# Gated delta rule in steps of 128 tokens instead of 64, in a hybrid mixer kernel

## The chip, the cores and the metric

The kernel runs on one core of one Trainium2 chip. The metric is the device time of one execution in microseconds (us); lower is better. The time before is 1988.86 us, the median of three runs (1986.17 to 1990.41).

## The reference

One layer of a decoder trunk works on 1024 tokens of width 1024. An input projection feeds five branches (gated DeltaNet, spatial gating, sparse attention, Mamba-2, cross-attention); their outputs are projected, gated and summed. The change lies in the first branch alone, in its gated delta rule, which has 4 heads of key and value width 128:

```
S_t = a_t S_{t-1} (I - b_t k_t k_t^T) + b_t v_t k_t^T,   o_t = S_t q_t
per chunk:  a_mat = I + tril(beta * (k k^T) * decay, -1)
            w_k, u0 = a_mat^-1 [beta * exp(gc) * k,  beta * v]
            u = u0 - w_k S;   o = (q * exp(gc)) S + (q k^T * decay) u
            S = exp(gc_last) S + (k * exp(gc_last - gc))^T u
```

Here gc is the running sum of the log decays within a chunk. The reference uses chunks of 64 tokens (16 of them); the recurrence itself does not depend on the size of the chunk.

## The kernel before, in words

Tokens lie in NT = 8 blocks of 128, and each block holds two chunks of 64, one in partitions 0 to 63 and one in 64 to 127 (E64). `branch_a` (L576) goes over the heads at L766. For each head there are these parts:

- `front(h)` (L614) makes the three projections q, k and v: each is 16 steps of three fp32r matmuls with 512 columns (`gin`), 48 steps in all, each projection followed by a convolution on ScalarE and VectorE. `proj_steps` is a generator, and `front(h+1)` is drawn on while head h is worked on: `feed(n)` (L623) issues n steps of three matmuls at that point of the program. For the last head the filling is `gate_steps(4)` (L567, tile `gate`), matmuls of the same form.
- `decays(h)` (L594) loads the rows of decays and betas by DMA on SyncE's queue (`dec`, `br`, `qd`, L598 to L601) and makes the factors of the chunk's matrix. `dec` has two buffers and `br` one of its own, so that the loads for the next head can come early.
- `mid(h)` (L623) first transposes and normalises q and k (L637 to L664), then makes the matrix U and its diagonal block inverse X with its transpose Y, and doubles the inverse four times (L687): each round is three groups of 16 matmuls of 64x64 (`prod`, L586; tiles `t`, `xt`, `t2y`), two at a time in opposite quarters of the array, with VectorE between them. L700 to L709 join the 32-token blocks into the transposed inverse `yb` of each 64-token chunk. L712 to L717 make `wk`.
- The scan (L722 to L741) takes 16 steps. Each step has five small products: `pu` from `yb` and `vb`, `pu` from `wk` and the state, `pst` from `kd` and `u`, `po` from `qd` and the state, `po` from `dec` and `u`; ScalarE copies `u` and `o`, and VectorE makes the next state `st` (L735). `feed(1)` stands behind the copy of `u`.
- `finish(h)` (L744) norms the output, makes one more projection (`a_gate`) and stores.

An fp32 product shows in the trace as two matmul instructions; an fp32r product is one.

The work is written as a dataflow; the framework that builds the program fixes the order of each engine's instructions beforehand, by their place in the program and by modelled times, and an instruction written later can be pulled forward into a place where its engine would stand idle. So `gate` matmuls that only head 3 draws stand in head 0 already. Within an engine's queue, and within SyncE's queue of DMA issues, the order is then fixed. The top-k rounds of the sparse attention (MAX8 and MATCH_REPLACE8 on VectorE) are spread over the VectorE instructions of branch a and of two later stages (`topk`, L474, with `share` at L1082), as work that fills gaps.

Of the kernel before, what the change touches and what calls it, by code (L numbers as in the profile page):

```python
# [15 lines left out]
P = 128  # L16
D = 1024
L = 1024
NT = L // P
# [36 lines left out]
def mixer_body(ctx, tc, a, out):  # L56
    nc = tc.nc
    S, G = nc.scalar, nc.gpsimd
    V, T = Traced(nc.vector), Traced(nc.tensor)
# [3 lines left out]
    px = ctx.enter_context(ExitStack())  # L63
# [10 lines left out]
    def gps(name, tag="g"):  # L74
        return pp.tile([P, 512], F32, name=name, tag=tag, bufs=banks[tag])

    def sps(name):
        return gps(name, "s")
# [91 lines left out]
    ekd = keep.tile([P, NT, 4], F32, name="ekd")  # L170
    cda = keep.tile([P, NT, 2, 4], F32, name="cda")
    btok = keep.tile([P, NT, 4], F32, name="btok")
    bte = keep.tile([P, NT, 4], F32, name="bte")
# [30 lines left out]
    HF = (slice(0, 4), slice(4, 8))  # L204

    def r3(t, c=P):
        return t.rearrange("p (n c) -> p n c", c=c)

    def flat(t):
        return t.rearrange("p n c -> p (n c)")  # L210

    def b3(ap, n, c=P):
        return ap[:, :, None].to_broadcast([P, n, c])
# [32 lines left out]
    with tc.tile_pool(name="xin", bufs=1, side="right") as xp:  # L246
# [6 lines left out]
        for b in range(8):  # L253
            ps = gps("gkvm", "f")
# [76 lines left out]
    def scores(name, q, j, kh, kl, c0, n):  # L331

        ps = sps(name)
        qj = q[:, j * P:(j + 1) * P]
        T.matmul(ps[:, :n], qj, kh[:, c0:c0 + n], start=True, stop=False)
        T.matmul(ps[:, :n], qj, kl[:, c0:c0 + n], start=False, stop=True)
        return ps
# [25 lines left out]
    with tc.tile_pool(name="idx", bufs=1, reuse_waits="tile") as ip:  # L363
        w = [split(*w_tiles("w"), raw[:, k:k + 4]) for k in (0, 4)]
        mraw = ip.tile([P, L], F32, name="mraw")
        for hv in HV:
            ps = gps("gmisc")
# [4 lines left out]
        z, sp, e, w, pl = r16("z"), r16("sp"), r16("e"), r16("w"), r16("pl")  # L372
# [24 lines left out]
        for hf in HF:  # L397
            ps = sps("ldT")
# [11 lines left out]
        ps = sps("csT")  # L410
# [6 lines left out]
        ps = sps("last")  # L417
# [17 lines left out]
        br = ip.tile([8, L], F32, name="br", tag="br")  # L435
# [12 lines left out]
        for c0 in range(0, L, 512):  # L448
            ps = sps("ikd")
# [4 lines left out]
        for b in range(4):  # L454
            th = stacks(ip, proj_in(OFF["c_iq"] + b * P), "iqs", 3)
            for j in range(NT):
                for hf in range(2):
                    h = 2 * b + hf
                    W = P * (j + 1)
                    for c0, n in cuts(W):  # L460
                        ps = scores("ix", th[hf], j, ikh, ikl, c0, n)
# [114 lines left out]
    def branch_a(gp):  # L576
        t3 = lambda nm, tg, b=1: gp.tile([P, NT, P], F32, name=nm, tag=tg, bufs=b)
        c3 = lambda nm, b=1: gp.tile([P, NT, 64], F32, name=nm, tag=nm, bufs=b)
        yb = t3("yb", "yb")
        G.memset(yb, 0.0)  # L580
        csv = csd.rearrange("r (j e c) -> r e j c", j=NT, e=2)
        btv = btd.rearrange("r (j e c) -> r e j c", j=NT, e=2)
        E64 = [slice(0, 64), slice(64, 128)]
# [8 lines left out]
        ready = []  # L592

        def decays(h):  # L594
            dec = c3("dec", 2)
            br = c3("br")
            for e in range(2):
                nc.sync.dma_start(dec[E64[e]], csv[h, e].partition_broadcast(64))  # L598
                nc.sync.dma_start(br[E64[e]], btv[h, e].partition_broadcast(64))
            qd = t3("qd", "qd")  # L600
            nc.sync.dma_start(flat(qd), egd[h].partition_broadcast(P))  # L601

            V.tensor_tensor(dec, dec, b3(cs[:, :, h], NT, 64), OP.subtract)
            nb = gp.tile([P, NT, 64], F32, name="nb", tag="T2c", bufs=1)
            V.tensor_scalar(nb, dec, 0.0, None, OP.max)
            V.tensor_scalar(dec, dec, 0.0, None, OP.min)
            S.activation(flat(nb), flat(nb), AF.Exp, scale=-1.0)
            S.activation(flat(dec), flat(dec), AF.Exp)
            G.tensor_tensor(br, br, dec, OP.mult)
            G.tensor_tensor(nb, nb, b3(btok[:, :, h], NT, 64), OP.mult)  # L610
            G.tensor_tensor(nb, nb, lv(0), OP.mult)
            return dec, br, nb, qd
# [10 lines left out]
        def mid(h, more, ch3, dec, br, nb, qd):  # L623
            def feed(n, after=False):
                with ExitStack() as x:
                    if after:
                        x.enter_context(tc.issue_after(T.log[-1]))
                    for _ in range(n):
                        next(more, None)
# [3 lines left out]
            rk = gp.tile([P, NT], F32, name="rk", tag="rk", bufs=2)  # L633
            kn = t3("kn", "T2")
            vb = t3("vb", "vb")
            kps = []
            for hf in HF:  # L637
                ps = tr4("kT", lambda i: ch3["k"][:, hf.start + i, :])
# [4 lines left out]
            for hf in HF:  # L643
                ps = tr4("vT", lambda i: ch3["v"][:, hf.start + i, :])
# [7 lines left out]
            knT = t3("knT", "knT")  # L652
            for hf in HF:
                ps = tr4("knTp", lambda i: kn[:, hf.start + i, :])
                S.activation(flat(knT[:, hf]), ps, AF.Copy)
            for hf in HF:
                ps = tr4("qT", lambda i: ch3["q"][:, hf.start + i, :])
# [5 lines left out]
            kd = t3("kd", "kd")  # L663
            G.tensor_tensor(kd, kn, b3(ekd[:, :, h], NT), OP.mult)  # L664

            U = c3("U")
            X, Y = c3("X"), c3("Y")
            idb = idl[:, None, :].to_broadcast([P, NT, 64])
            ps = sps("kk")
            prod(ps, lambda j, e: knT[:, j, e], lambda j, e: knT[:, j, e])  # L670
            V.tensor_tensor(flat(U), ps, flat(br), OP.mult)
            V.tensor_tensor(X, r3(ps, 64), nb, OP.mult)
            V.tensor_tensor(X, idb, X, OP.subtract)
            V.tensor_tensor(Y, U, lv(6), OP.mult)
            V.tensor_tensor(Y, idb, Y, OP.subtract)
            feed(1)
            ps = sps("kq")
            prod(ps, lambda j, e: knT[:, j, e], lambda j, e: ch3["q"][:, j, e])
            V.tensor_tensor(flat(dec), ps, flat(dec), OP.mult)
            for e in E64:  # L680
                G.affine_select(dec[e], dec[e], pattern=[[0, NT], [1, 64]], compare_op=OP.is_ge, fill=0.0, base=0, channel_multiplier=-1)
            for hf in HF:
                V.tensor_tensor(qd[:, hf], qd[:, hf], ch3["q"][:, hf], OP.mult)
            feed(1)

            T2 = c3("T2c")
            for k in range(1, 5):  # L687
                ps = sps("t2")
                prod(ps, lambda j, e: U[e, j, :], lambda j, e: X[e, j, :])
                V.tensor_tensor(T2, r3(ps, 64), lv(k), OP.mult)  # L690
                feed(2)
                px = sps("xt2")
                prod(px, lambda j, e: Y[e, j, :], lambda j, e: T2[e, j, :])
                py = sps("t2y")
                prod(py, lambda j, e: T2[e, j, :], lambda j, e: Y[e, j, :])
                V.tensor_tensor(flat(X), flat(X), px, OP.subtract)
                V.tensor_tensor(flat(Y), flat(Y), py, OP.subtract)
                feed(2, h < 2)

            Q = [(slice(0, 32), slice(32, 64)), (slice(64, 96), slice(96, 128))]  # L700
            ps, py = sps("t2"), sps("t2y")
            for i, (e, (r0, r1)) in enumerate(zip(E64, Q)):
                S.activation(yb[e, :, e], Y[e], AF.Copy)
                for j in range(NT):
                    T.matmul(ps[r1, j * 32:(j + 1) * 32], U[r0, j, 32:64], X[r0, j, 0:32], start=True, stop=True)
                S.activation(T2[r1, :, 0:32], r3(ps[r1, 0:256], 32), AF.Copy)
                for j in range(NT):
                    T.matmul(py[r0, j * 32:(j + 1) * 32], T2[r1, j, 0:32], Y[r1, j, 32:64], start=True, stop=True)
                V.tensor_tensor(yb[r0, :, r1], Y[r0, :, 32:64], r3(py[r0, 0:256], 32), OP.subtract)  # L709
            feed(2)  # L710

            wk = t3("wk", "knT")  # L712
            for hf in HF:
                ps = sps("wkp")
# [4 lines left out]
            st = gp.tile([P, P], F32, name="st", tag="st", bufs=2)  # L719
            G.memset(st, 0.0)  # L720
            o = t3("o", "T2")
            for n in range(16):  # L722
                j, ei = divmod(n, 2)
                e = E64[ei]
                pu = sps("pu")
                T.matmul(pu[e, 0:P], yb[e, j, e], vb[e, j, :], start=True, stop=False)
                T.matmul(pu[e, 0:P], wk[:, j, e], st, start=False, stop=True)
                u = gp.tile([P, P], F32, name="u", tag="u", bufs=2)
                S.activation(u[e], pu[e, 0:P], AF.Copy)
                feed(1)  # L730
                if n < 15:
                    pst = sps("pst")
                    T.matmul(pst[:, 0:P], kd[e, j, :], u[e], start=True, stop=True)
                    s2 = gp.tile([P, P], F32, name="st", tag="st", bufs=2)
                    V.scalar_tensor_tensor(s2, st, cda[:, j, ei, h:h + 1], pst[:, 0:P], OP.mult, OP.add)  # L735
                po = sps("po")
                T.matmul(po[e, 0:P], qd[:, j, e], st, start=True, stop=False)
                T.matmul(po[e, 0:P], dec[e, j, :], u[e], start=False, stop=True)
                S.activation(o[e, j, :], po[e, 0:P], AF.Copy)
                if n < 15:  # L740
                    st = s2  # L741
            return o, rq

# [360 lines left out]
    fill = []  # L1104
# [229 lines left out]
    with tc.tile_pool(name="fo", bufs=1, reuse_waits="tile") as fo:  # L1334
# [8 lines left out]
        for j in range(4):  # L1343
            tok = [slice((j + 4 * i) * P, (j + 4 * i + 1) * P) for i in range(2)]
            base = []
# [33 lines left out]
```

## Time and profile before

| | |
|---|---|
| median of 3 runs | 1988.86 us |
| the profiled execution's own time | 1991.76 us |
| its span, first to last instruction | 1989.8 us |
| TensorE busy / weight load busy | 95% / 75% |
| VectorE / ScalarE / GpSimd busy | 77% / 39% / 27% |
| mean granted TensorE clock | 0.986 |
| head 0 of branch a: preparing and inverse, scan, finish | 203.20 to 254.58, to 299.30, to 313.50 us |
| scans of heads 1, 2, 3 | 362.00 to 406.30, 462.30 to 508.30, 563.80 to 608.80 us |

How to read it: PE is TensorE's matmuls, PEld its weight loads (which overlap with matmuls), DVE is VectorE, ACT ScalarE, POOL GpSimd, SPq the DMA issues of SyncE. A matmul's shown duration is longer than what it occupies of the engine, since matmuls are pipelined; what a run of them occupies is read from the distance of their starts. Nearly all matmuls and VectorE instructions are recorded under L50, a line of the helper that logs them, so the tile names tell them apart.

### The profile page before, as it was taken

To read this page: it belongs to the slowest core of one execution; us is meant where nothing else is said; L and a number is where in the kernel's file an instruction comes from. 1 tells how busy PE (TensorE), PEld (TensorE's weight loads), DVE (VectorE), ACT (ScalarE), POOL (GpSimd) and SP (SyncE) were. 2 spreads that over 40 slices of the span, in tenths; PEclk is the share of its full clock that TensorE was granted. 3 is DMA by queue.
4 is the path that set the end of the run, shared out by engine and by line. 5 is a ranking of instruction groups with operands and counts; after the bars stand their busy time and mean duration, and the time that the engine had idled before them with its cause. 6 is when DMAs were issued, how large, how long until landed. Compare 5 with 4: busy or idle time off the path is not lost.

```text
span 1989.8 us, 30429 instructions
## 1 busy us (share of the span) xinstructions
PE 1885.3 (95%) x11116; PEld 1486.7 (75%) x11116; DVE 1533.0 (77%) x2699; ACT 780.9 (39%) x1511; POOL 545.6 (27%) x513
## 2 busy tenths in 40 slices
PE   6999999999999999969999999999989989999888
PEld 5777757676667787758888888888867667887767
DVE  7678958686846899798777787777787758897874
ACT  6465332323223341334222233343333737764231
POOL 5102202020200313443222222222115254444134
PEclk9999999999999999979999999999999999999999
DMA  6413102020202221233333333333368363324533
GB/s 191 116 48 70 44 17 59 17 60 17 61 31 69 53 55 48 85 100 117 106 106 117 111 111 108 109 113 112 108 219 288 126 188 104 97 86 139 170 110 132
DMA packets 187910, 199.89 MB, mean 100 GB/s; under 512 B 23641, under 2 KB 139214, under 8 KB 187762
## 3 DMA queue, kind: packets, MB, share of 16 engines
q1 hardware_dynamic: 187186, 196.91, 32.1%
q8 instruction: 88, 1.44, 0.3%
q10 hardware_dynamic: 576, 1.05, 0.1%
q14 instruction: 60, 0.49, 0.1%
HBM read 141.67 MB, written 52.05 MB: 97 GB/s over the span
## 4 chain that ended last, share of the span: by engine, by line
PE 68%; DVE 12%; issue 4%; DMA 3%; POOL 2%; ACT 2%; SPq 0%; POOLq 0%; DVEq 0%; ACTq 0%
PE pm L50 30%; PE gin L50 12%; PE proj L50 6%; PE po L50 4%; PE gate L50 2%; PE lg L50 2%; PE pT L50 2%; DVE cacc L50 1%; PE pu L50 1%; PE pst L50 1%; PE t L50 1%; DMA yr<-yd 1%; PE t2y L50 1%; DVE sc L50 1%; DVE m L50 1%
## 5 line engine op out<-in xcount | busy, mean ns | idle before, releaser
L50 PE MATMUL proj<-part,whi 128*128 128x512 f32 x640 | 210.6, 404 | 8.2 <-DVE tgl L50 3.1
L50 DVE MAX8 m<-sc 128x8 f32<-128x384 f32 (+5 forms) x192 | 170.4, 888 | 1.6
L50 DVE MATCH_REPLACE8 sc<-m,sc 128x384 f32<-128x384 f32 (+5 forms) x192 | 168.1, 876 | 0.0
L105 ACT ACTIVATE fh<-fs 128x512 fp32r<-128x512 f32 x132 | 83.1, 632 | 193.6 <-PE pm L50 187.8
L50 PEld LDWEIGHTS proj<-part,whi 128*128 128x128 f32 x640 | 121.1, 192 | 34.9 <-DVE tgl L50 4.6
L50 PE MATMUL proj<-part,wlo 128*128 128x512 f32 x320 | 128.8, 403 | 4.8 <-DVE wlo L50 4.8
L50 DVE SCALAR_TENSOR_TENSOR u<-pm,u 128x512 f32<-128x512 f32 x128 | 85.0, 684 | 47.5 <-PE pm L50 47.2
L105 ACT ACTIVATE whi<-wraw 128x512 fp32r<-128x512 f32 x106 | 66.4, 629 | 138.3 <-PE gin L50 88.9
L105 ACT ACTIVATE fh<-gr 128x512 fp32r<-128x512 f32 x90 | 56.8, 632 | 146.4 <-PE pm L50 115.3
L50 DVE TENSOR_TENSOR fl<-fs,fh 128x512 fp32r<-128x512 f32 x132 | 93.8, 713 | 3.5 <-ACT fh L105 3.5
L1154 POOL TENSOR_TENSOR fs<-gr 128x512 f32<-128x512 f32 x30 | 38.9, 1297 | 184.7 <-DVE fl L50 182.2
L1300 POOL TENSOR_TENSOR mg<-mg,tgl 128x512 f32<-128x512 f32 x48 | 67.9, 1417 | 57.4 <-DVE tgl L50 51.0
L50 DVE TENSOR_TENSOR fl<-gr,fh 128x512 fp32r<-128x512 f32 x90 | 64.1, 713 | 24.5 <-ACT fh L105 24.5
L50 DVE SCALAR_TENSOR_TENSOR cacc<-craw,pc,cacc 128x1023 f32<-128x1023 f32 (+2 forms) x60 | 77.6, 1294 | 6.3 <-ACT cacc L543 5.9
L50 DVE TENSOR_TENSOR wlo<-wraw,whi 128x512 fp32r<-128x512 f32 x82 | 59.6, 731 | 29.4 <-ACT whi L105 19.5
L50 DVE SCALAR_TENSOR_TENSOR st<-st,cda,pst 128x128 f32<-128x128 f32 x60 | 20.8, 347 | 74.4 <-PE pst L50 74.3
L50 PEld LDWEIGHTS proj<-part,wlo 128*128 128x128 f32 x320 | 61.2, 191 | 17.1 <-DVE wlo L50 5.2
L1153 POOL TENSOR_TENSOR fs<-gr 128x512 f32<-128x512 f32 x30 | 39.5, 1317 | 117.3 <-issue 117.3
L877 ACT ACTIVATE lg<-lg,mx,rq 128x128 f32<-128x128 f32 (+7 forms) x64 | 54.9, 861 | 18.5 <-DVE mx L50 16.3
L50 DVE SCALAR_TENSOR_TENSOR lg<-sc,cf,lg 128x384 f32<-128x384 f32 (+3 forms) x96 | 56.3, 605 | 6.9 <-POOL cf L856 3.8
L50 PE MATMUL pm<-h00h,fl 128*128 128x512 f32 x120 | 47.8, 398 | 12.4 <-DVE fl L50 12.4
L50 DVE SCALAR_TENSOR_TENSOR sc<-rl,iwt,sc 128x512 f32<-128x512 f32 (+3 forms) x84 | 47.1, 615 | 13.1 <-ACT rl L463 11.8
(579 smaller groups left out, 5714.1 us busy)
## 6 DMA issues: line engine op xcount, KB each, us to landing
tgl<-gd SPq DMA_DIRECT2D x80, 256.0 KB, 3.0
wraw<-in_w_in_dram SPq DMA_DIRECT2D x66, 256.0 KB, 2.9
gr<-in_w_gate_dram SPq DMA_DIRECT2D x32, 512.0 KB, 3.6
gr<-in_w_in_dram SPq DMA_DIRECT2D x28, 512.0 KB, 3.8
yr<-yd SPq DMA_DIRECT2D x40, 256.0 KB, 3.8
wraw<-in_w_branch_dram SPq DMA_DIRECT2D x40, 256.0 KB, 3.9
yd<-sg SPq DMA_DIRECT2D x16, 512.0 KB, 3.1
gd<-u SPq DMA_DIRECT2D x30, 256.0 KB, 3.8
```

Of the source, the lines that this page charges most:

```text
L50: r = f(*args, **kw)
L105: S.activation(hi, raw, AF.Copy)
L877: S.activation(lg[:, :W], lg[:, :W], AF.Exp, scale=rq[:, 2 * j + hf:2 * j + hf + 1], bias=mx[:, hf:hf + 1], accum_out=sm[:, hf:hf + 1])
L1153: eng.tensor_tensor(s3, a11, a21, OP.subtract)
L1154: eng.tensor_tensor(s1, a21, a22, OP.add)
L1300: (G if n < 4 else V).tensor_tensor(m, m, t, OP.add)
```

## The change

The scan goes over the 8 blocks of 128 tokens. The two 64-token chunks of a block become one chunk of 128, for which these things are needed:

- The factors `bte`, `ekd` and the block's decay `cdc` become products of the two chunks' decays (five small VectorE instructions, once).
- The lower left quarter of the inverse of the 128-token matrix (its transpose stands in the upper right quarter of `yb`): a further doubling, of two groups of 8 unpaired 64x64 products with VectorE's factor between them and a ScalarE copy behind, and 8 more 32x32 products that complete X.
- The products of the second chunk's queries and keys with the first chunk's keys (`px`, 16 products of 128x64, put into round 3 of the doubling), scaled on VectorE into `dq` (128x128 per block, takes the place of `dec` in the scan) and `UX`.
- `qd` of the second chunk is multiplied by the first chunk's decay, on GpSimd.
- `dec` keeps one buffer instead of two, and X shares the one buffer of `br` (tag `br`).
- `feed` is called with 2 in each of the 8 steps of the scan instead of with 1 in each of 16, and with 2 at two more places behind the joining.

```
     def branch_a(gp):
-        yb = t3("yb", "yb")
+        yb, dq = t3("yb", "yb"), t3("dq", "dq")
         G.memset(yb, 0.0)
+        G.memset(dq, 0.0)
+        hbt, hkd, cdc = [gp.tile([P, NT, 4], F32, name=nm) for nm in ("hbt", "hkd", "cdc")]
+        V.tensor_copy(hbt, bte)
+        V.tensor_copy(hkd, ekd)
+        V.tensor_tensor(bte[64:128], hbt[64:128], cda[64:128, :, 0, :], OP.mult)
+        V.tensor_tensor(ekd[0:64], hkd[0:64], cda[0:64, :, 1, :], OP.mult)
+        V.tensor_tensor(cdc, cda[:, :, 0, :], cda[:, :, 1, :], OP.mult)
...
-            dec = c3("dec", 2)
+            dec = c3("dec")
...
-            U = c3("U")
-            X, Y = c3("X"), c3("Y")
+            e0, e1 = E64
+            U, UX, Y = c3("U"), c3("UX"), c3("Y")
+            X = gp.tile([P, NT, 64], F32, name="X", tag="br", bufs=1)
...
-                G.affine_select(dec[e], dec[e], pattern=[[0, NT], [1, 64]], ...)
-            for hf in HF:
-                V.tensor_tensor(qd[:, hf], qd[:, hf], ch3["q"][:, hf], OP.mult)
+                G.affine_select(dq[e, :, e], dec[e], pattern=[[0, NT], [1, 64]], ...)
...
+            hk = hkd[e0, :, h:h + 1].to_broadcast([64, NT, 64])
             for k in range(1, 5):
+                if k == 2:
+                    for hf in HF:
+                        V.tensor_tensor(qd[:, hf], qd[:, hf], ch3["q"][:, hf], OP.mult)
+                if k == 3:
+                    px = sps("kqx")
+                    for j in range(NT):
+                        T.matmul(px[e0, j * 64:(j + 1) * 64], knT[:, j, e0], qd[:, j, e1], start=True, stop=True)
+                        T.matmul(px[e1, j * 64:(j + 1) * 64], knT[:, j, e0], knT[:, j, e1], start=True, stop=True)
+                    V.tensor_tensor(dq[e0, :, e1], r3(px, 64)[e0], hk, OP.mult)
+                    V.tensor_tensor(UX[e0], r3(px, 64)[e1], hk, OP.mult)
+                    G.tensor_tensor(qd[:, :, e1], qd[:, :, e1], b3(cda[:, :, 0, h], NT, 64), OP.mult)
...
+                if i == 0:
+                    for j in range(NT):
+                        T.matmul(py[r1, j * 32:(j + 1) * 32], Y[r1, j, 32:64], T2[r1, j, 0:32], start=True, stop=True)
+                    S.activation(X[r1, :, 0:32], r3(py[r1, 0:256], 32), AF.Copy, scale=-1.0)
...
+            feed(2)
+            ps = sps("t2")
+            for j in range(NT):
+                T.matmul(ps[e1, j * 64:(j + 1) * 64], UX[e0, j, :], X[e0, j, :], start=True, stop=True)
+            V.tensor_tensor(T2[e1], r3(ps, 64)[e1], hbt[e1, :, h:h + 1].to_broadcast([64, NT, 64]), OP.mult)
+            feed(2)
+            py = sps("t2y")
+            for j in range(NT):
+                T.matmul(py[e0, j * 64:(j + 1) * 64], T2[e1, j, :], yb[e1, j, e1], start=True, stop=True)
+            S.activation(yb[e0, :, e1], r3(py, 64)[e0], AF.Copy, scale=-1.0)
             feed(2)
...
-            for n in range(16):
-                j, ei = divmod(n, 2)
-                e = E64[ei]
+            for n in range(NT):
                 pu = sps("pu")
-                T.matmul(pu[e, 0:P], yb[e, j, e], vb[e, j, :], start=True, stop=False)
-                T.matmul(pu[e, 0:P], wk[:, j, e], st, start=False, stop=True)
+                T.matmul(pu[:, 0:P], yb[:, n, :], vb[:, n, :], start=True, stop=False)
+                T.matmul(pu[:, 0:P], wk[:, n, :], st, start=False, stop=True)
                 u = gp.tile([P, P], F32, name="u", tag="u", bufs=2)
-                S.activation(u[e], pu[e, 0:P], AF.Copy)
-                feed(1)
-                if n < 15:
+                S.activation(u, pu[:, 0:P], AF.Copy)
+                feed(2)
+                if n < NT - 1:
                     pst = sps("pst")
-                    T.matmul(pst[:, 0:P], kd[e, j, :], u[e], start=True, stop=True)
+                    T.matmul(pst[:, 0:P], kd[:, n, :], u, start=True, stop=True)
                     s2 = gp.tile([P, P], F32, name="st", tag="st", bufs=2)
-                    V.scalar_tensor_tensor(s2, st, cda[:, j, ei, h:h + 1], pst[:, 0:P], OP.mult, OP.add)
+                    V.scalar_tensor_tensor(s2, st, cdc[:, n, h:h + 1], pst[:, 0:P], OP.mult, OP.add)
                 po = sps("po")
-                T.matmul(po[e, 0:P], qd[:, j, e], st, start=True, stop=False)
-                T.matmul(po[e, 0:P], dec[e, j, :], u[e], start=False, stop=True)
-                S.activation(o[e, j, :], po[e, 0:P], AF.Copy)
+                T.matmul(po[:, 0:P], qd[:, n, :], st, start=True, stop=False)
+                T.matmul(po[:, 0:P], dq[:, n, :], u, start=False, stop=True)
+                S.activation(o[:, n, :], po[:, 0:P], AF.Copy)
```

## Rows read from the trace of the kernel before

**Rows 1.** The page's first part: busy us, share of the span, instructions.

```profile
PE 1885.3 (95%) x11116; PEld 1486.7 (75%) x11116; DVE 1533.0 (77%) x2699; ACT 780.9 (39%) x1511; POOL 545.6 (27%) x513
```

**Rows 2.** Busy time by stretch: head 0's inverse, then the four scans.

```profile
core 0: us, PE busy (x) PEld busy (x) DVE busy (x) ACT busy (x) POOL busy (x), PEclk, DMA share, GB/s
203.20:254.58 51.38, 49.83 (x667) 40.33 (x667) 45.55 (x88) 15.85 (x28) 11.03 (x7) 1.00 0.16 43
254.58:299.30 44.72, 44.72 (x222) 23.90 (x221) 21.75 (x48) 15.08 (x42) 3.01 (x4) 1.00 0.07 19
362.00:406.30 44.30, 44.30 (x221) 23.88 (x221) 22.51 (x45) 15.83 (x44) 2.97 (x4) 1.00 0.08 18
462.30:508.30 46.00, 45.98 (x228) 24.83 (x227) 28.99 (x60) 15.62 (x43) 3.77 (x4) 1.00 0.07 18
563.80:608.80 45.00, 45.00 (x223) 24.01 (x223) 14.29 (x31) 13.44 (x40) 0.00 (x0) 1.00 0.11 36
```

**Rows 3.** The scans, filling alone: four rows of tile gin, then one of gate.

```profile
254.58:299.30 44.72, 23.30 (x65) 10.24 (x65) 0.00 (x0) 2.44 (x4) 1.00 0.07 19
362.00:406.30 44.30, 22.91 (x64) 10.25 (x65) 0.00 (x0) 2.61 (x5) 1.00 0.08 18
462.30:508.30 46.00, 24.53 (x71) 11.21 (x71) 0.00 (x0) 2.33 (x4) 1.00 0.07 18
563.80:608.80 45.00, 4.70 (x13) 2.16 (x14) 0.00 (x0) 0.00 (x0) 1.00 0.11 36
...
563.80:608.80 45.00, 18.55 (x51) 8.01 (x51) 1.77 (x3) 1.00 0.11 36
```

**Rows 4.** Timeline of TensorE, one scan step of head 0: start, duration, what.

```profile
258.81 0.48 PE L50 MATMUL pst<-u,kd 64*128 64x128 f32 x2
259.23 0.43 PE L50 MATMUL po<-st,qd 128*64 128x128 f32 x2
259.59 0.32 PE L50 MATMUL po<-u,dec 64*64 64x128 f32 x1
259.60 0.32 PE L50 MATMUL pu<-vb,yb 64*64 64x128 f32 x1
...
259.96 0.50 PE L50 MATMUL gin<-h01h,wlo 128*128 128x512 f32 x1
...
260.62 0.43 PE L50 MATMUL pu<-st,wk 128*64 128x128 f32 x2
...
261.64 0.48 PE L50 MATMUL pst<-u,kd 64*128 64x128 f32 x2
```

**Rows 5.** Timeline of TensorE, head 0 ahead of the scan: five places.

```profile
193.34 0.39 PE L50 MATMUL gin<-h00l,whi 128*128 128x512 f32 x1
...
195.83 0.39 PE L50 MATMUL gin<-h10h,whi 128*128 128x512 f32 x1
...
216.64 1.15 PE L50 MATMUL kk<-knT 128*64 128x64 f32 x32
...
245.81 0.69 PE L50 MATMUL t<-X,U 32*32 32x32 f32 x16
...
252.69 1.96 PE L50 MATMUL wkp<-yb,kb 128*128 128x128 f32 x16
```

**Rows 6.** Weight loads by tile: duration in ns min/median/max, first and last start.

```profile
L50 PEld LDWEIGHTS pu<-st,wk x32: 132/134/136, 254.9 to 298.2; 128*64 128x64 f32 x32
...
L50 PEld LDWEIGHTS wkp<-yb,kb x16: 187/192/192, 252.6 to 254.3; 128*128 128x128 f32 x16
```

**Rows 7.** Timeline of VectorE: one product of the inverse, one state update.

```profile
223.18 0.68 DVE L50 TENSOR_TENSOR T2c<-t,lvl 128x512 f32<-128x512 f32 x1
...
259.34 0.35 DVE L50 SCALAR_TENSOR_TENSOR st<-st,cda,pst 128x128 f32<-128x128 f32 x1 [2.25 <-PE pst L50]
```

**Rows 8.** Timeline of SyncE's DMA issues in head 0.

```profile
180.10 1.26 SPq L598 DMA_DIRECT2D dec<-csd  x2
...
219.07 1.26 SPq L599 DMA_DIRECT2D br<-btd  x2
...
235.00 0.37 SPq L120 DMA_DIRECT2D wraw<-in_w_in_dram  x1
```

More of the change, by code (lines that the diff above doesn't have):

```diff
@@ L680, in mid @@
             for e in E64:
-                G.affine_select(dec[e], dec[e], pattern=[[0, NT], [1, 64]], compare_op=OP.is_ge, fill=0.0, base=0, channel_multiplier=-1)
-            for hf in HF:
-                V.tensor_tensor(qd[:, hf], qd[:, hf], ch3["q"][:, hf], OP.mult)
+                G.affine_select(dq[e, :, e], dec[e], pattern=[[0, NT], [1, 64]], compare_op=OP.is_ge, fill=0.0, base=0, channel_multiplier=-1)
             feed(1)
             T2 = c3("T2c")
+            hk = hkd[e0, :, h:h + 1].to_broadcast([64, NT, 64])
             for k in range(1, 5):
+                if k == 2:
[9 more added lines that the diff above has]
+                    G.tensor_tensor(qd[:, :, e1], qd[:, :, e1], b3(cda[:, :, 0, h], NT, 64), OP.mult)
                 ps = sps("t2")
@@ L721, in mid @@
             o = t3("o", "T2")
-            for n in range(16):
-                j, ei = divmod(n, 2)
-                e = E64[ei]
+            for n in range(NT):
                 pu = sps("pu")
-                T.matmul(pu[e, 0:P], yb[e, j, e], vb[e, j, :], start=True, stop=False)
-                T.matmul(pu[e, 0:P], wk[:, j, e], st, start=False, stop=True)
+                T.matmul(pu[:, 0:P], yb[:, n, :], vb[:, n, :], start=True, stop=False)
+                T.matmul(pu[:, 0:P], wk[:, n, :], st, start=False, stop=True)
                 u = gp.tile([P, P], F32, name="u", tag="u", bufs=2)
-                S.activation(u[e], pu[e, 0:P], AF.Copy)
-                feed(1)
-                if n < 15:
+                S.activation(u, pu[:, 0:P], AF.Copy)
+                feed(2)
+                if n < NT - 1:
                     pst = sps("pst")
-                    T.matmul(pst[:, 0:P], kd[e, j, :], u[e], start=True, stop=True)
+                    T.matmul(pst[:, 0:P], kd[:, n, :], u, start=True, stop=True)
                     s2 = gp.tile([P, P], F32, name="st", tag="st", bufs=2)
-                    V.scalar_tensor_tensor(s2, st, cda[:, j, ei, h:h + 1], pst[:, 0:P], OP.mult, OP.add)
+                    V.scalar_tensor_tensor(s2, st, cdc[:, n, h:h + 1], pst[:, 0:P], OP.mult, OP.add)
                 po = sps("po")
-                T.matmul(po[e, 0:P], qd[:, j, e], st, start=True, stop=False)
-                T.matmul(po[e, 0:P], dec[e, j, :], u[e], start=False, stop=True)
-                S.activation(o[e, j, :], po[e, 0:P], AF.Copy)
-                if n < 15:
+                T.matmul(po[:, 0:P], qd[:, n, :], st, start=True, stop=False)
+                T.matmul(po[:, 0:P], dq[:, n, :], u, start=False, stop=True)
+                S.activation(o[:, n, :], po[:, 0:P], AF.Copy)
+                if n < NT - 1:
                     st = s2
```

## The prediction, made before the changed kernel ran

> **What bounds the kernel now.** I read the engines' busy shares first: TensorE is busy 95% of the span, VectorE 77% [rows 1]. A busy TensorE proves little by itself, since its matmuls overlap, so the next view was the stretches of branch a. In the four scans TensorE is covered without a gap (44.72 of 44.72 us in head 0, 45.98 of 46.00 at worst), at a granted clock of 1.00, the 2.4 GHz level; VectorE has 22 of 45 us there, ScalarE 15 [rows 2]. So the scan waits for TensorE. The third view counts what of the scan is filling, which has to be done somewhere anyway: 65, 64, 71 and 64 (13 + 51) matmuls with 512 columns, 264 in all [rows 3]. In an undisturbed run such matmuls start 0.226 us apart (11 distances between 193.34 and 195.83 us) [rows 5]. The scans take 180.0 us together (the sum of their lengths) [rows 2]; less 264 x 0.226 = 59.7 that leaves 120.3 us which the 64 steps themselves cost, 1.88 us a step.
>
> The fourth view, the timeline of one step, shows where the 1.88 goes [rows 4]. Each product is a pair of instructions. The pair of `pst` holds the engine 0.42 us (258.81 to 259.23), the pair of `po` from the state 0.36, the last pair of `po` and the first of the next `pu` 0.36 together, since they lie in opposite quarters of the array and start 0.01 us apart, and `pu` from the state, between the filling, about 0.36. That is 1.50; the rest, 0.4, is that filling broken into groups of two costs more than 0.226 each. Against this stands `wkp`, a run of the same fp32 kind in the full 128x128 shape: 16 instructions in 1.96 us, less the tail of the last (some 0.27), 0.1125 each, 0.225 a pair [rows 5].
>
> **The change, part by part.** *Scan.* 64 steps become 32, each with five pairs in the shape of `wkp`. No two of them can now lie beside each other; the pair that was free is paid for. The trace has no step of this kind, so I bound it. From above: every pair costs as much as `pst`'s, 0.42 (it too loads 128 columns), and the filling keeps its 0.4: 2.5 us a step, 80 in all, a gain of 40. From below: 10 x 0.1125 and 0.1 for one group of filling, 1.22 us, 39 in all, a gain of 81. I take `wkp`'s 0.1125, the row whose shape and type are the same, so 1.12; 0.2 for two groups of filling; and 0.35 for a new wait: the next state is ready 0.53 us after `pst` starts plus 0.35 on VectorE [rows 4, 7], 0.9 with the hand-over, and behind `pst` now stand only three pairs that need no new state (0.225 each, 0.9 with `pst`'s own). Any VectorE instruction of 0.7 us that stands ahead of the update shows, unless filling is pulled in between. The sum is 1.67 us a step, 53 in all: **67 us gained**.
>
> In the step now, every pair changes the shape of the array against its neighbour (64x128, 128x64, 64x64, then 128x128 filling), while from filling to `wkp` no shape changes [rows 4, 5]. The Trainium skill, TensorEngine Tiling (Array Packing), Key Properties, says that changing the tiling mode drains TensorE; by it the extra 0.1 to 0.2 of a pair would go with the shapes and the sum stays with `wkp`'s price, while pairs that wait for ScalarE or VectorE would keep it.
>
> *Inverse.* Per head TensorE gets: `px`, 32 instructions of `kk`'s form, 1.0 (1.15 with the tail); 16 of 32x32, 0.6 (0.69 with the tail) [rows 5]; two groups of 16 of 64x64 that have no partner in another quarter. An alone one costs at least what the 32x32 ones cost (0.6 the group) and at most as much as a pair of them beside each other (32 of `kk` in 1.0): I take 0.9 each, 1.8. Three more groups break the filling, some 0.2 each as in the scan, 0.6. That is 4.0. Behind the two new groups stand a VectorE product (0.68 [rows 7]) and a ScalarE copy, each covered by six matmuls of filling, 1.4 us; I allow 0.5 a head for lateness. Together 4.5 a head, **18 us lost**; ends 3 and 7.5 a head, 12 and 30.
>
> *Other engines, at nothing.* VectorE gains three products of 0.68 a head (half the partitions, the same columns) and loses eight updates of 0.35 [rows 7]: 2.0 against 2.8. ScalarE loses sixteen copies and gains two, with 15 of 45 us used; GpSimd gains one product with 11 of 51 us used [rows 2]. If ScalarE's cover failed, the copy of `yb` would hold `wkp` for a good half us a head. The five small VectorE instructions at the start lie beside head 0's projections; without that cover they cost 1 us once. The filling that is drawn earlier is only moved: it was in the scan or behind it, and TensorE has it to do in either place.
>
> *DMA order.* `dec` and `br` for the next head were issued at 180.10 and 219.07 us, more than 30 us ahead of the scan [rows 8]. Now `dec` can only follow the masks, and `br` the last use of X, at about the start of `wkp` (252.7). They are needed in the next head's inverse, after this scan, which shrinks to some 28 us, so the delay is hidden as such. What is queued behind them on SyncE is the next weight load (235.00) [rows 8].
>
> **Sum.** 67 less 18 is 49 us. The profiled execution took 1991.76 us (span 1989.8 and 2.0 around it), 2.9 above the median of the runs; 1942.8 against it, and 1988.9 - 49 = **1940 us** for the median.
>
> **Rivals.** *1. Pairs keep their price* (2.5 us a step): every pair follows a semaphore, and a weight load of 128 columns takes 192 ns against 134 for 64 [rows 6]. Gain 40 - 18 = 22: 1967 us. For it: `pst`, with 128 columns, is the dearest pair. Against it: `wkp`'s loads of 192 ns are hidden at 0.1125. The Trainium skill, TensorE: Matmul & The Clock Gate, LDWEIGHTS, lets a load's time go with its columns alone, which the two rows bear out; were the loads on the path, this rival would be the result. Chance 0.18, with values from 1955 to 1972.
>
> *2. VectorE takes part of it back in the inverse*, where it is busy 45.55 of 51.38 us [rows 2]. The scan has 21.75 - 15 x 0.35 = 16.5 us of other VectorE work, mostly top-k rounds, which are laid out over branch a's VectorE instructions; the scan will hold half as many of these. If 8.3 us of it move into the inverse with the 2.0 of new products, they exceed its 5.8 us of room by 4.5 a head, 18 in all: 31 gained, 1958 us. Against it: rounds that find no room can be done later, in the scan. Chance 0.10.
>
> *3. Slower: SyncE's queue.* If `br`'s load for the next head keeps its early place in the order, ahead of the weight load of 235.00, it waits there until X is free, and the load behind it goes out at about 254, 19 us late. TensorE would run out of filling, and three heads (the last one loads no successor) lose up to 57 us: 1940 + 57 = 1997 us. It turns slower once more than 16 us a head are lost. Against it: the order is planned with that wait known, so the load should be placed behind. Chance 0.05.
>
> *4. Nothing moves*, because losses of the second and third kind just eat the gain, or the output's chain at each head's end is what sets its length. Against it: TensorE is filled in the scan without a gap. Chance 0.04.
>
> A gain of more than 62 us, with one group of filling a step and no wait, has 0.05; the forecast (1926 to 1955) has 0.58.
>
> **How the numbers follow.** The range 1924 to 1972 holds the forecast and the first two rivals. It leaves out the largest gains, the small ones and the slower cases, somewhat under 2 in 10. Differences within 0.2% (4 us), about what a measurement of this kernel tells from none, count as the same: 0.04. Slower 0.05, faster 0.91.
>
> **What would show it.** In the changed profile the scans should be about 28 us long each with 50 to 65 matmuls of filling, no pair above 0.25 us between its starts except where it waits, and `pst` followed within 0.9 us by the next state's `pu` or by filling. The inverse should be 4 to 5 us longer at the same filling. Rival 1 shows as pairs 0.36 to 0.42 apart; rival 2 as waits of `xt`, `t2y` or `wkp` for VectorE; rival 3 as gaps on TensorE ended by a late `whi` or `wlo`. All stages after branch a should keep their lengths; if one grows by over 5 us, the sum is wrong in a place that I did not look at.

## The result, and the profile after

The changed kernel takes 1929.59 us (median of four runs, 1928.29 to 1930.53) against 1989.63 for the kernel before on the same chip: a ratio of 0.970, interval 0.9684 to 0.9717, 60 us gained. The forecast was 1940, the range 1924 to 1972. The executions that left the two traces have spans of 1926.6 and 1989.8 us, 63.2 apart; the account below is made between these.

The first line is the page's own, of the kernel after; it answers to [rows 1]. TensorE has lost 66 us of shown busy time with the same number of instructions.

```profile
PE 1819.6 (94%) x11116; PEld 1490.7 (77%) x11116; DVE 1535.1 (80%) x2684; ACT 765.1 (40%) x1455; POOL 546.0 (28%) x518
```

Next, the kernel after by stretch: for each head the preparing and inverse (from its first `kT`), then the scan (to its last `po`). The columns are those of [rows 2].

```profile
core 0: us, PE busy (x) PEld busy (x) DVE busy (x) ACT busy (x) POOL busy (x), PEclk, DMA share, GB/s
203.82:260.98 57.16, 57.16 (x756) 46.48 (x757) 51.41 (x99) 17.14 (x30) 12.14 (x8) 0.97 0.16 43
260.98:280.62 19.64, 18.91 (x120) 16.23 (x119) 14.16 (x29) 9.19 (x24) 3.01 (x4) 1.00 0.11 28
296.59:353.46 56.87, 52.78 (x743) 42.41 (x742) 51.43 (x99) 15.03 (x27) 10.91 (x8) 1.00 0.17 48
353.46:371.65 18.19, 18.19 (x116) 15.46 (x115) 12.69 (x23) 8.96 (x24) 2.72 (x3) 1.00 0.06 15
387.63:437.44 49.81, 46.86 (x721) 38.37 (x720) 44.70 (x83) 14.14 (x25) 11.52 (x9) 1.00 0.16 44
437.44:457.49 20.05, 20.05 (x127) 17.52 (x125) 18.18 (x37) 9.33 (x24) 2.40 (x3) 1.00 0.11 27
473.48:524.47 50.99, 47.40 (x719) 39.35 (x717) 42.68 (x72) 11.14 (x21) 10.48 (x7) 0.97 0.19 58
524.47:539.23 14.76, 14.73 (x99) 11.85 (x97) 6.18 (x14) 5.76 (x18) 0.00 (x0) 1.00 0.05 19
```

The scans last 15 to 20 us instead of 44 to 46, and the inverses 50 to 57 instead of 42 to 51. Both are misread without the filling, whose place has moved too. (The `...` in a fence marks rows left out.) The scans' filling, tile `gin` and then `gate`, as in [rows 3]:

```profile
260.98:280.62 19.64, 12.09 (x41) 6.98 (x41) 0.00 (x0) 2.44 (x4) 1.00 0.11 28
353.46:371.65 18.19, 11.20 (x37) 6.23 (x37) 0.00 (x0) 2.44 (x4) 1.00 0.06 15
437.44:457.49 20.05, 13.51 (x47) 8.11 (x47) 0.00 (x0) 2.56 (x4) 1.00 0.11 27
...
524.47:539.23 14.76, 6.82 (x19) 3.08 (x19) 0.60 (x1) 1.00 0.05 19
```

That is 144 matmuls where 264 were. With 0.226 us for each, 72.6 - 144 x 0.226 = 40 us are left for the scans themselves, against some 121 before. The inverses held 371 fillings against 338 before. Their lengths, and the busy time of each engine in them, add up to these two sums, after and before:

```profile
sum 214.83, PE 204.20 PEld 166.61 DVE 190.23 ACT 57.45 POOL 45.06; mean PE 51.05 PEld 41.65 DVE 47.56 ACT 14.36 POOL 11.26
```

```profile
sum 184.07, PE 177.39 PEld 144.05 DVE 165.06 ACT 49.71 POOL 40.26; mean PE 44.35 PEld 36.01 DVE 41.26 ACT 12.43 POOL 10.06
```

Net of filling (2.49 us over 11 distances, 0.2264 each) that is 130.8 and 107.5 us. The three ends between a scan and the next head's `kT`, net in the same way, went from 8.0 to 3.1. So: scans -81, inverses +23, ends -5, together -63, which is the whole difference of the spans. What follows branch a is 6 us longer (1376.0 to 1381.9 from the last `po` to the last matmul), since 32 fillings fewer were done by then (713 for 745), which is 7 us of work.

The 23 us of the inverses are not all work. TensorE stands idle in them for 10.6 us (214.83 less 204.20), before for 6.7 (184.07 less 177.39). And the clock of 0.97 in two of the rows is two stretches of 3.4 us in which TensorE was granted the lower level, 1.2 GHz; before there is none:

```profile
204.30:207.70 3.40, 3.40 (x13) 2.81 (x12) 3.40 (x7) 1.84 (x4) 0.00 (x0) 0.51 0.41 95
477.50:480.80 3.30, 3.30 (x13) 2.73 (x12) 2.65 (x6) 0.63 (x1) 1.17 (x1) 0.50 0.40 159
```

Matmuls of filling start 0.43 us apart in the second (479.45 to 479.88) instead of 0.226, so about half of these 6.8 us, 3.4, is lost by estimate. That leaves some 16 of the 23 us as added work and some 7 as waits and slow clock. The slow stretches did not lengthen the kernel: a second trace of it (`c1_after_again`, below) has one, in head 1's inverse instead of those of heads 0 and 3, and its four inverses are as long as these within 0.03 us, with 12.1 us idle. TensorE waits less where it is slow.

VectorE's part has moved as well: 25 us more of its work lie in the inverses (165.06 to 190.23 us busy) and 36 us less in the scans (87.5 to 51.2, from [rows 2] and the rows above).

One step of the scan after, in TensorE's timeline (start, duration), answers to [rows 4]:

```profile
267.40 0.38 PE L50 MATMUL pst<-u,kd 128*128 128x128 f32 x2
267.62 0.39 PE L50 MATMUL po<-st,qd 128*128 128x128 f32 x2
267.84 0.39 PE L50 MATMUL po<-u,dq 128*128 128x128 f32 x2
268.07 0.39 PE L50 MATMUL pu<-vb,yb 128*128 128x128 f32 x2
268.29 0.42 PE L50 MATMUL pu<-st,wk 128*128 128x128 f32 x2
268.47 0.47 PE L50 MATMUL gin<-h00h,whi 128*128 128x512 f32 x1
...
269.94 0.38 PE L50 MATMUL pst<-u,kd 128*128 128x128 f32 x2
```

The pairs follow each other at 0.22 us, where they held the engine 0.36 to 0.42 before, and here `pu` from the new state starts 0.89 us after `pst` with nothing between but the three pairs that need no state. Over the 28 such steps of the four scans that distance is 0.89 to 1.00 us in 18 steps without filling between, and 1.17 to 2.05 us in the other 10, where one to five matmuls of filling stand between.

### The profile page after: what moved, and what is told of

Its sections match the earlier page's. It is cut to its first block, busy times and chain, and to the rows that moved or that the text cites. A ratio compares the mean times of both kernels' runs of the same rounds, so it can differ in the third digit from the quotient of the medians.

```text
span 1926.6 us, 30311 instructions
## 1 busy us (share of the span) xinstructions
PE 1819.6 (94%) x11116; PEld 1490.7 (77%) x11116; DVE 1535.1 (80%) x2684; ACT 765.1 (40%) x1455; POOL 546.0 (28%) x518
## 4 chain that ended last, share of the span: by engine, by line
PE 71%; DVE 16%; issue 4%; DMA 3%; ACT 3%; POOL 2%; SPq 0%; POOLq 0%; DVEq 0%; ACTq 0%
PE pm L50 31%; PE gin L50 13%; PE proj L50 8%; PE po L50 3%; PE lg L50 2%; PE gate L50 2%; DVE sc L50 2%; PE pT L50 2%; PE ix L50 2%; DVE m L50 1%; DVE cacc L50 1%; PE t L50 1%; PE t2y L50 1%; DVE wlo L50 1%; DVE lm L50 1%
## 5 line engine op out<-in xcount | busy, mean ns | idle before, releaser
L50 PEld LDWEIGHTS proj<-part,whi 128*128 128x128 f32 x640 | 120.6, 191 | 34.4 <-DVE tgl L50 4.0
L922 ACT ACTIVATE pt<-pT 128x512 f32<-128x512 f32 (+3 forms) x96 | 43.1, 484 | 34.1 <-PE po L50 25.9
```

Source lines behind the costliest of these rows:

```text
L50: r = f(*args, **kw)
L922: S.activation(pt[:, i0 * P:(i0 + n) * P], ps[:, :n * P], AF.Copy)
```

## The experiments

Two theories of where the scan's gain comes from stood against each other: the shape of the products (A) or the number of steps (B). Two runs were made to part them, one each way. A first group of four ran on one chip, where the kernel before took 1992.56 us; times are compared through the ratio to it.

**The shape alone.** The kernel before with full-shape products, but still 64 steps (the products of `po` likewise; `dec`, which the scan no longer reads, has one buffer as in the change):

```
+        yb, dq = t3("yb", "yb"), t3("dq", "dq")      # dq zeroed, masks write its diagonal blocks
+        uz = [gp.tile([P, P], F32, name=f"u{i}") for i in range(2)]    # zeroed once
...
-                T.matmul(pu[e, 0:P], yb[e, j, e], vb[e, j, :], start=True, stop=False)
+                T.matmul(pu[:, 0:P], yb[:, j, :], vb[:, j, :], start=True, stop=False)
...
-                    T.matmul(pst[:, 0:P], kd[e, j, :], u[e], start=True, stop=True)
+                    T.matmul(pst[:, 0:P], kd[:, j, :], u, start=True, stop=True)
```

> The kernel before, with its 64 steps of 64 tokens, but every product of the scan in the full 128x128 shape (the unused half of u is zero, the masked products stand in a block-diagonal 128x128 tile). Theory A: what made a pair dear in the scan was the change of the array's shape from pair to pair; with one shape all through a pair costs 0.225 us, a step without its filling 1.25 instead of 1.90, the four scans lose 64 x 0.65 = 41 us: 1949 us (1943 to 1955), although no step was saved. Theory B: a pair is dear because each one waits for another engine, and the gain of the change came from half the steps alone: the step stays at 1.9 us, and the two pairs that ran beside each other now run one behind the other, 0.36 more: 1990 to 2012 us.

Measured: 1951.23 us, 0.9794 of before (0.9778 to 0.9811), 41 us gained with not one step fewer, inside what theory A gives and far from theory B. TensorE's timeline of this kernel shows a step:

```profile
258.37 0.49 PE L50 MATMUL pst<-u,kd 128*128 128x128 f32 x2
258.70 0.39 PE L50 MATMUL po<-st,qd 128*128 128x128 f32 x2
258.92 0.39 PE L50 MATMUL po<-u,dq 128*128 128x128 f32 x2
259.14 0.39 PE L50 MATMUL pu<-vb,yb 128*128 128x128 f32 x2
259.37 0.42 PE L50 MATMUL pu<-st,wk 128*128 128x128 f32 x2
```

The same products wait for ScalarE and VectorE, and the pairs are 0.22 us apart but for `pst` behind its wait (0.33). The four scans (127.71 us with 185 fillings) cost 85.8 us net of filling, 1.34 a step, against 1.9. Part of the array multiplies zeros or makes results that nobody reads, and it is faster. Of the 41 us, 35 are in the scans; 5 more are in the three heads' ends, which are at 3.0 us net as in the changed kernel, while the inverses stay at 107.9. So the shorter ends come neither from fewer steps nor from the added doubling; what shortens them was not tried.

That splits the 81 us of the scans: 35 with the shape alone, the other 46 (85.8 to 40.0) with half the steps in that shape. No run halved the steps in the old shapes.

**The shape put back.** The changed kernel with two products of each step cut in two:

```
-                T.matmul(pu[:, 0:P], wk[:, n, :], st, start=False, stop=True)
+                for e in E64:
+                    T.matmul(pu[e, 0:P], wk[:, n, e], st, start=False, stop=True)
...
-                T.matmul(po[:, 0:P], qd[:, n, :], st, start=True, stop=False)
+                for e in E64:
+                    T.matmul(po[e, 0:P], qd[:, n, e], st, start=True, stop=False)
```

> The changed kernel with two of the five products of each step (pu and po from the state) cut into two halves of 128x64 that lie beside each other in the array; the arithmetic is the same. Theory A: a step then changes the shape up to four times, at 0.1 to 0.15 us each, 32 steps: 13 to 19 us slower than the changed kernel, 1943 to 1949 us, and the pairs beside these products 0.3 to 0.4 us apart. Theory B: shapes cost nothing, 1930 us within 3.

Measured: 1949.35 us, 0.9783 (0.9765 to 0.98), which is 0.0083 above the changed kernel's 0.970, 16.5 us. Its timeline:

```profile
267.80 0.38 PE L50 MATMUL pst<-u,kd 128*128 128x128 f32 x2
268.12 0.44 PE L50 MATMUL po<-st,qd 128*64 128x128 f32 x4
268.49 0.49 PE L50 MATMUL po<-u,dq 128*128 128x128 f32 x2
268.81 0.39 PE L50 MATMUL pu<-vb,yb 128*128 128x128 f32 x2
269.13 0.44 PE L50 MATMUL pu<-st,wk 128*64 128x128 f32 x4
269.50 0.50 PE L50 MATMUL gin<-h11h,whi 128*128 128x512 f32 x1
```

Every group is now 0.32 to 0.37 from the next, also `po` from `u` behind the halves, which the edit did not touch and which waits for nothing new; it is followed by a pair of its own shape, so the price of a change shows beside it too, and not only in the distance across it. The scans (90.25 us with 144 fillings) cost 57.6 us net instead of 40.0: 17.6 us for 32 steps of four changes, 0.14 us a change. The halves also bring four more instructions a step, which this run doesn't part from the shapes; the run before has no instruction more or less than its kernel before. There, by estimate, six changes a step went [rows 4] and one pair of 0.225 us that had been free was paid for: 1.88 less 1.34, plus 0.225, is 0.77, or 0.13 us a change. Theory A holds in both directions.

**The doubling alone.** The changed kernel without what was added to the inverse (the `px` products with what uses them, the 8 products of 32x32, and the two groups of 64x64 with their VectorE product and ScalarE copy):

> The changed kernel without the added doubling: the products of the second chunk with the first chunk's keys, the 32x32 products that complete X, and the two groups of 64x64 products with what VectorE, ScalarE and GpSimd do for them are left out, so the coupling of the two chunks of a block is missing from the output; the three places of filling stay. Prediction's term: the doubling costs 4.5 us a head, 18 us; read from the stretches of the changed profile 18.6 (inverse 23.5 longer net of filling, heads' ends 4.9 shorter): 1911 us (1906 to 1914). Rival: the chain of waits around it would set the inverse's length anyway, and under 10 us come back: over 1920.

Measured: 1917.57 us, 0.9621 (0.9607 to 0.9636): 15.7 us less than with it, between the two expectations and nearer to the first. Its inverses hold 347 fillings:

```profile
sum 197.27, PE 182.80 PEld 148.68 DVE 177.94 ACT 52.35 POOL 44.58; mean PE 45.70 PEld 37.17 DVE 44.49 ACT 13.09 POOL 11.14
```

That is 118.7 net, 12.1 less than the changed kernel's; 11 of the 23 us stay when the doubling is gone. They are no work: TensorE is idle for 14.5 us here (197.27 less 182.80), 7.8 more than in the kernel before, and two stretches at the 1.2 GHz level in head 3 lose another 3.4 by estimate. So 16 us of work gave back 12 in the inverses, since TensorE then waits longer. Its longest waits from 200 to 560 us in this kernel (who waits, for whom, us in all, times, longest; `t` is the first product of a doubling round, `vT` and `knTp` are transposes at a head's start, `sg` the product at the end of the head before):

```profile
PE t L50 <- DVE X L50: 5.4, 2, 2.7
PE vT L50 <- DVE sg L50: 5.4, 3, 1.9
PE knTp L50 <- DVE kn L50: 2.0, 2, 1.0
```

All are for VectorE, which does the same work in less time. The kernel before has 3.2 us of such waits at the heads' ends too (`oT` for `o`), which are gone.

**The buffers alone.** The kernel before with one buffer for `dec` and X in the buffer of `br`:

```
-            dec = c3("dec", 2)
+            dec = c3("dec")
...
-            X, Y = c3("X"), c3("Y")
+            Y = c3("Y")
+            X = gp.tile([P, NT, 64], F32, name="X", tag="br", bufs=1)
```

> The kernel before with the change's buffers alone: one buffer for dec, and X in the buffer of br. If the later loads of the next head's decays hold up nothing, as I costed them: 1989.6 us within 3. If they hold SyncE's queue and the weight loads behind them (the third rival of the prediction): slower by up to 57 us, with TensorE waiting for late weights in the inverse.

Measured: 1999.24 us, 1.0033 (1.0018 to 1.0048): 6.6 us slower, so neither expectation. The queue of SyncE was not it; the order put `br`'s load at 247.67 us, behind X. What grew is TensorE's wait at the heads' ends for `o`, the normed output, 4.4 us of it at the end of head 0; from 200 us to the end of branch a, the kernel before and then this one:

```profile
PE oT L50 <- DVE o L50: 3.2, 3, 1.2
PE oT L50 <- DVE o L50: 9.5, 5, 4.4
```

In the scan before, `dec` itself is an operand to the last step, so with one buffer its next load goes out at 299.7 us, and the factors' work on VectorE and GpSimd falls into the end of the head, ahead of the norm of the output: `ro`'s power on GpSimd waits there behind two products of `nb`. The three ends took 15.7 us net instead of 8.0; the traced execution (2004.73 us) is 5.5 us above the median, and TensorE has stretches at the lower clock in it (0.91 of full in head 0's end), so the wait, 6.3 us more, is the surer figure. In the changed kernel the same sharing does not do this, since the scan reads `dq`, and `dec` is free when the masks are done: its load goes out at 225.56 us, in the inverse, and its ends are at 3.1. So the sharing had a price that the rest of the change removes. That the price is `dec`'s and not X's is read from the trace; no run took the two apart.

The second group of four ran beside a kernel before of 1993.06 us, the changed kernel among them again:

> The changed kernel as it is, for comparison on the same chip with the three runs beside it: 0.970 of the kernel before, within 0.002.

Measured: 1932.64 us, 0.9696 (0.9677 to 0.9716).

**Fewer top-k rounds in branch a.**

```
-    share = {"a": 0.3, "d": 0.1, "t": 0.6}
+    share = {"a": 0.2, "d": 0.1, "t": 0.7}
```

> The changed kernel with fewer top-k rounds laid out over branch a (a fifth of them instead of three tenths; the rest go to the later stage of the gates). Theory: of the inverse's 23 us that it grew by, 12 are the doubling's work (the run without it shortened the inverse by 12.1) and 11 are waits for VectorE, which has the same work in less time: vT for sg, knTp for kn, the first t for X. With a third of the rounds gone from there they fall by about half: 1924 us on the first chip's scale, 0.967 of before. Rival: the waits are the chain's own length and not the rounds': unchanged, or slower by up to 5 us as the gates' stage has 34 us more VectorE work.

Measured: 1923.49 us, 0.9648 (0.9632 to 0.9665), nearly twice the gain expected. Its profiled execution (1928.13 us; the three others 1923.3 to 1923.6) does not show where, since TensorE was granted the lower clock for 13.6 us of it, so it was repeated below, where the gain is the 6 us expected.

**Less filling drawn in the scan** (`feed(2)` to `feed(1)` in the step):

> The changed kernel with one step of filling (three matmuls) instead of two in each step of the scan. Theory: a step's own chain (copy of u, state update) takes 0.7 to 0.9 us on each side and is covered by 3 to 5 matmuls of filling and by the pairs that need no new state; the planner pulls filling forward anyhow, and what is not drawn here comes behind the scan, so the time stays within 3 us of the changed kernel. Rival: the filling drawn here is what hides the chain; with less of it each of 32 steps shows 0.2 to 0.5 us: 6 to 16 us slower.

Measured: 1932.95 us, 0.9696 (0.9681 to 0.9711), the same as the changed kernel. The scans cost 42.2 us net instead of 40.0; what was not drawn there came behind the scan (66 fillings at an end became 77 to 90).

**Other banks for the output's transposes.**

```
-                ps = tr4("oT", lambda i: o[:, hf.start + i, :])
+                ps = gps("oT", "f")
+                for i in range(4):
+                    T.transpose(ps[:, i * P:(i + 1) * P], o[:, hf.start + i, :], ident)
```

> The changed kernel with the output's transposes (oT) in the two PSUM banks of the gates' products instead of the four small ones. The transposes of v (vT) then need not wait for the banks that sg's last product on VectorE sets free: three gaps of 2.1 to 2.5 us on TensorE at the heads' starts. Theory: 4 to 6 us faster than the changed kernel. Rival: the gates' filling is held up instead, or the wait moves to the next place where VectorE is late (knTp for kn): within 2 us, or slower.

Measured: 1951.04 us, 0.9784 (0.9767 to 0.9801), 17.5 us slower than the changed kernel beside it. The wait of `vT` for `sg` went, but so did the gates' filling: the inverses of heads 0 and 1 hold not one `gate` matmul, where the changed kernel has 30 and 12, and TensorE waited longer for VectorE in the same places:

```profile
PE knTp L50 <- DVE kn L50: 7.4, 3, 3.3
PE vT L50 <- DVE chv L50: 4.7, 1, 4.7
PE t L50 <- DVE X L50: 3.6, 4, 2.4
```

The rival held: in the inverses TensorE is idle for 20.4 us instead of 12.1, and the stages behind branch a are 11 us longer than in the changed kernel beside it. It shows how much of the inverse is covered by filling that can be pulled forward.

**How far the rounds can go, and whether it is the change's doing.** A last group beside a kernel before of 1994.58 us: a tenth of the rounds in branch a (shares 0.1, 0.1, 0.8), the kernel before with a fifth, and the fifth again.

> The changed kernel with a tenth of the top-k rounds laid out over branch a. If what the fifth gained (0.9648 of before against 0.9696) came from VectorE's queue in branch a, a further step gains again, but less, since the waits that are left there are of its own chain, and the gates' stage, whose VectorE was busy 460 of 560 us with the fifth, fills up: 0.962 to 0.966. Rival: the gates' stage turns the bound and the gain is given back: 0.968 or more.

> The kernel before with a fifth of the top-k rounds over branch a. If VectorE is in the way only since the change (the same work in 60 us less), the kernel before hardly moves: 0.998 to 1.002 of before. Rival: it was in the way already, and the gain has nothing to do with the change: 0.994 to 0.996.

> The changed kernel with a fifth of the rounds once more, since its first profile held some 20 us in which TensorE was granted less than its full clock in head 3: 0.965 of before within 0.002, and an inverse of the four heads that is, net of filling, 5 to 9 us shorter than the changed kernel's 130.8.

Measured: the tenth 1918.88 us, 0.963 (0.9611 to 0.9648); the kernel before with a fifth 0.9984 (0.9969 to 1.0), so hardly moved; the fifth again 0.9665 (0.9639 to 0.9691), its inverses 126.9 us net, 4 shorter and not quite the 5 to 9 expected. The two runs of the fifth gain 10 and 6 us on the changed kernel, and the second interval overlaps that kernel's (0.9677 to 0.9716). TensorE's waits from 200 to 560 us, first the changed kernel, then the one with a tenth:

```profile
PE vT L50 <- DVE sg L50: 5.8, 3, 2.1
PE kT L50 <- DVE chk L50: 2.2, 1, 2.2
PE t L50 <- DVE X L50: 2.2, 2, 1.3
PE knTp L50 <- DVE kn L50: 2.0, 2, 1.1
```

```profile
PE knTp L50 <- DVE kn L50: 2.2, 3, 0.7
PE vT L50 <- DVE chv L50: 1.3, 1, 1.3
PE vT L50 <- DVE sg L50: 0.5, 1, 0.5
```

Twelve us of waits became four, and the inverses (359 fillings) fell from 130.8 to 120.6 us net:

```profile
sum 201.88, PE 197.79 PEld 161.95 DVE 141.64 ACT 57.55 POOL 45.62; mean PE 49.45 PEld 40.49 DVE 35.41 ACT 14.39 POOL 11.41
```

TensorE is idle for 4.1 us in them, at its full clock throughout. Less these, 116.5 us are left, 15.6 more than the kernel before has in the same way (107.5 less 6.7): the doubling's work once more. The stage that takes the rounds over holds them: VectorE is busy 486 of the 560 us from 900 to 1460, and TensorE 551.

```profile
900.00:1460.00 560.00, 551.03 (x2480) 454.83 (x2479) 486.44 (x764) 186.66 (x310) 149.48 (x118) 0.99 0.40 132
```

So the changed kernel with a tenth of the rounds in branch a is the fastest of those that ran, 13 us below the changed kernel by the ratios (0.963 against 0.9696, intervals apart). The kernel before was not tried with a tenth, so how much of the 13 us is the change's doing is shown only for the step to a fifth: 3 us before (0 to 6), 6 to 10 after it.

## Why the prediction was right, and by how much it missed

*The bound.* That the scan waits for TensorE, and that its own cost is to be counted net of filling, was right: the scans fell by 81 us of TensorE's time, and the spans by 63.

*The scan's step.* The prediction chose `wkp`'s 0.1125 an instruction for the pairs, because shape and type are the same [rows 5], and that was right: 0.22 a pair. The two experiments with the shape show why. The Trainium skill, TensorEngine Tiling (Array Packing), Key Properties, says that a change of the tiling mode drains the engine; the traces fit that, with a price of 0.13 to 0.14 us a change, though they show the time and not the draining. Mis-sized was the term of 0.35 us a step "for a new wait": it is not there. The wait is as long as I reckoned, 0.9 us from `pst` to the next state; but the four pairs behind `pst`'s start hold TensorE just as long, in 10 of 28 steps filling stands between, the exception that the prediction itself named; and in all four scans the waits of 0.2 us or more come to 0.7 us, once, for the first copy of `u`. A step cost 1.25 us (40 / 32) and not 1.67. This is 13 of the 14 us by which the sum (49) fell short of the spans' 63; it came out at the end of the bounds that I had called "from below", 39 us.

*The inverse.* 4.5 us a head, 18 in all, was the forecast. Inverse and ends together took 18.4 (23.3 less 4.9). That this meets the 18 is in part luck: the doubling's own work is some 16 us, close to the prediction's 4.0 a head, but the waits and the slower clock of TensorE grew by some 7 and not by 0.5 a head, and the heads' ends, which the forecast didn't touch, gave 5 back. The 7 us are the mechanism of the second rival, at under half of its price of 18, and not mainly through the new products: by the prediction's 2.0 us a head these are 8 of the 25 us that VectorE got more in the inverses. The unpaired group of 64x64 took 1.07 us (344.95 to 346.02), a little over the upper bound of 1.0 and not the 0.9 I took.

*Other engines and buffers, at nothing.* For VectorE this was wrong: the prediction weighed its sums of work, which hardly changed, and not where the work falls, in the inverses. For the buffers it was right in the changed kernel, but for a reason that I did not give: alone, the sharing of buffers cost 6.6 us, in the heads' ends, where the prediction looked only at SyncE's queue and at whether the loads are early enough.

*The rivals.* The first (pairs keep their price, 1967) fell: the pairs of the scan cost what `wkp`'s do, 0.11 us an instruction, and loads shown as 192 ns do not lengthen that. "Hidden" was still too strong a word for them. The Trainium skill, TensorE: Matmul & The Clock Gate, LDWEIGHTS, gives a load's time by its columns alone, P / 1.2 ns, by estimate 107 ns for 128. The traces agree on the columns (130 and 134 ns shown for 64 of them with 64 and 128 rows, 184 and 192 for 128), but each shown load is some 80 ns longer than the formula's. Later in the kernel before, a run of `pyd`, with 128 weight columns but only 64 moving columns, also has its instructions 0.11 us apart (674.21 to 674.54 us), so the loads may well be what sets this price; no run parts the two. The third (SyncE's queue) fell: in the changed kernel `br`'s load stands at 254.13 us, behind X, and the weight loads went out at 235.62 as before [rows 8]. The fourth fell with the result.

*Signs foretold.* Scans of 28 us with 50 to 65 fillings were foretold, and 15 to 20 with 19 to 47 came: with the step shorter, the planner put more of the filling elsewhere. The inverses are 5.8 us a head longer net of filling, where 4 to 5 were foretold. The stages behind grew by 6 us, over the 5 that I had set; that is the filling not yet done, 7 us, and no loss.

## What to carry to other kernels

Small fp32 products of mixed shapes in a row pay for each change of shape, here over half as much as for a whole pair; before saving steps or work, try to bring all of them, zeros included, into one shape (41 us here with no step saved, 35 of them in the scans). Count a stage net of the work that merely fills it, by a row for one such piece, or its length misleads in both directions. And after the bound engine has lost work, look at the engine that now has the same work in less time: here taking a third of the top-k rounds out of branch a, nearly indifferent before (0.9984), became worth 6 to 10 us, and taking two thirds out 13.

## What was not expected of the hardware

One change of the array's shape cost 0.13 to 0.14 us in the scans (17.6 us for 128 changes in the run with the halves). TensorE's granted clock can fall inside a stretch that it fills to the end: in the first profile with a fifth of the rounds it was at half, the 1.2 GHz level, for 13.6 us. The first row below is that stretch, the second the whole of head 3's inverse in that execution, the third the same inverse in the repeat, with the same 716 matmuls:

```profile
508.30:521.90 13.60, 13.60 (x75) 10.65 (x73) 2.13 (x4) 2.57 (x5) 0.00 (x0) 0.50 0.14 40
468.92:522.80 53.88, 51.36 (x716) 42.17 (x714) 35.34 (x63) 11.25 (x21) 11.73 (x7) 0.87 0.18 56
470.09:518.01 47.92, 45.40 (x716) 37.57 (x714) 35.33 (x63) 11.26 (x21) 11.74 (x7) 1.00 0.20 62
```

The slow stretch cost 6.0 us there, and that execution was 4.7 us longer than its three fellows, while the two stretches of 3.4 us in the changed kernel, in inverses where TensorE waits for VectorE anyway, cost nothing. Ahead of the fall, from 469 to 500 us, TensorE was busy 28.5 of 31 us at its full clock, and from 500 to 508.3 all the time. What made it fall was not tried.
